# Projection sums of the state-space stage copied out of three PSUM banks by ScalarE

## The chip, the cores and the metric

The kernel runs on 1 core of one Trainium2 chip. The metric is the device time of one execution in microseconds; of several runs the median counts. Engines are named TensorE (PE in the profile, PEld for its weight loads), VectorE (DVE), ScalarE (ACT), GpSimd (POOL) and SyncE (SP, which issues DMAs).

## The reference

One layer of a hybrid decoder: an S5 state-space branch and a dilated-window attention branch work side by side on the same normalised input, for a prompt of 1024 rows and for 8 x 4 decode rows with a cache of 1024 keys.

```python
def _layer(h, h0_re, h0_im, attend, norm_in_g, w_in, ...):
    proj = _rmsnorm(h, norm_in_g) @ w_in            # (rows, 1024) @ (1024, 3072)
    x_s, z_s = proj[..., :o1], proj[..., o1:o2]     # 512 columns each, as the four below
    q, k, v, z_a = proj[..., o2:o3], proj[..., o3:o4], proj[..., o4:o5], proj[..., o5:]
    y_s, st_re, st_im = _s5_scan(x_s, h0_re, h0_im, A_re, A_im, log_dt, B_re, B_im, C_re, C_im, D)
    gl = gelu(y_s) @ w_glu + b_glu
    y_s = gl[..., :D_SSM] * sigmoid(gl[..., D_SSM:])
    y_s = _rmsnorm(y_s * silu(z_s), norm_ssm_g)
    y_a = _rmsnorm(attend(qh, kh, vh) * silu(z_a), norm_attn_g)
    return h + concatenate([y_s, y_a], axis=-1) @ w_out, kh, vh, st_re, st_im
```

The prompt's keys and values, the decode rows' keys and values, and the final states are outputs too (`k_prompt` is one of them).

## The kernel before

The first stage, from 0 to about 318 us, loads x, projects it with most of `w_in` and runs the state-space scan. Its instructions are ordered by a scheduler that simulates the engines and emits, engine by engine, one queue; what stands in the program text in another order may be interleaved. The later stages (rest of the projections, decode attention, prompt attention, output projection) are ordered by hand.

**PSUM.** In the first stage the eight banks are divided by use (L113): two for projection sums ("mm"), two for transposes ("tp"), two for the sums of the scan ("ss") and two for its outputs ("so"). A tile of a use takes the bank that was used longest ago, and its first matmul waits for the last reader of what lay there.

**Exact products by splitting.** The helper `split` makes of a value a rounded high part (ScalarE, L139 or L142) and the remainder (VectorE, L140 or L143). A product of two values is three matmuls: high x high, high x low, low x high.

**x load.** Eight chunks of 128 rows of the prompt, then 32 decode rows (`xd`), are normalised (ScalarE's square sum, VectorE's short root, GpSimd's scaling) and turned: four transposes by TensorE into a "tp" bank (L274; L281 for the decode rows), the high part by ScalarE, the remainder by VectorE, both from the bank into `xT`. Between the turns TensorE runs L294, the first weight block, whose matmuls use each chunk as it comes. Over the same stretch VectorE and ScalarE work out the constants of the scan (L429 to L555: powers, sines, the matrices bb and bbw).

**Projection.** Blocks of 256 columns of `w_in` are loaded, scaled and split into eight tiles `win`, in a pool of twelve buffers (L142 on ScalarE, L143 on VectorE). A block of state-space inputs, gates, queries or keys is two half blocks of 128 columns by three column ranges of 352: six sums of 24 matmuls each (L314), each 128 x 352 in one "mm" bank. Of a gate sum ScalarE takes a tanh (L341) and VectorE multiplies (L342; L344 for the decode columns of the first range), both reading the bank. Of a query or key sum ScalarE takes the high part (L378), VectorE the remainder (L379), a third copy goes to `k_prompt` for keys (L384), and all read the bank. The decode columns are copied to `pdT` (L363) and later turned into a "tp" bank (L405). The blocks in the order of the scan's steps are `((0, 1), (1, None), (2, 5), (3, 2), (4, 3), (5, 7), (6, 4), (7, 9))`, the pair being a step and the block that goes with it: 0 and 1 are state-space inputs, 2 and 3 gates, 4 and 5 queries, 7 keys, 8 and 9 values.

**Scan.** Eight steps run between the sums. A step's matrix `wa` is made by GpSimd and VectorE (L598), turned ("tp", L602) and split (`wl`); products with `uhl` fill "ss" banks; VectorE and GpSimd rotate and scan them (L644 to L677: `rc`, `rs`, `zz`, `zs`, `xx`); the splits `xhl`, `fhl`, `thl` feed the output sums L688 ("so").

Of the kernel before, what the change touches and what calls it, by code (L numbers as in the profile page):

```python
# [10 lines left out]
F32 = mybir.dt.float32  # L11
F32R = mybir.dt.float32r
I32 = mybir.dt.int32
AF = mybir.ActivationFunctionType
# [7 lines left out]
DB, DS = 8, 4  # L22
# [81 lines left out]
def hymba_kernel(ctx: ExitStack, tc: tile.TileContext, I, O):  # L104
    nc = tc.nc
    V, S, GP, T, SY = nc.vector, nc.scalar, nc.gpsimd, nc.tensor, nc.sync
# [3 lines left out]
    st = ctx.enter_context(tc.tile_pool(reuse_waits="tile", name="st", bufs=2))  # L110
    pst = ExitStack()
    ps = [pst.enter_context(tc.tile_pool(reuse_waits="tile", name="ps", bufs=1, space=PSUM))]
    banks = {"mm": 2, "tp": 2, "ss": 2, "so": 2}  # L113
    dr = ctx.enter_context(tc.tile_pool(reuse_waits="tile", name="dr", bufs=1, space=DRAM))

    def ps_tile(shape, tag, dt=F32):
# [2 lines left out]
    def mm_ps(shape):  # L119
        return ps_tile(shape, "mm")  # L120

    def tp_ps(shape):
        return ps_tile(shape, "tp")
# [10 lines left out]
    def f(t):  # L134
        return t.bitcast(F32)
# [74 lines left out]
    sp = pa.enter_context(tc.tile_pool(reuse_waits="tile", name="sp", bufs=1))  # L210
# [23 lines left out]
    with tc.tile_pool(reuse_waits="tile", name="xin", bufs=6) as xp:  # L234
# [15 lines left out]
        p = mm_ps([128, 512])  # L250
# [6 lines left out]
        pw = p  # L257
        for i in range(8):
# [11 lines left out]
            for h in range(2):  # L270
                p = tp_ps([128, 4, 128])
# [7 lines left out]
        p = tp_ps([128, 8, 32])  # L279
# [30 lines left out]
    def proj_t(p, w, c, x):  # L310
        n = 0
        for kt in range(8):
            for a, b in PASSES:
                T.matmul(p, w(b, kt)[:, c * 128:c * 128 + 128], x(a, kt), start=(n == 0), stop=(n == 23))  # L314
                n += 1

    def in_proj_s(reg, half, w):

        for c in range(2):
            ct = 2 * half + c  # L320

            t = sp.tile([128, 8, W + DB], F32, tag="stp", name="stp", bufs=2)
            if reg == 0:
                GP.memset(t[:, DS:, NC:W], 0.0)
                GP.memset(t[:, :DS, W:], 0.0)
            for k in range(3):
                p = mm_ps([128, 512])[:, :352]
                proj_t(p, w, c, lambda a, kt: xT[a][:, kt, 352 * k:352 * k + 352])
                d = 0 if k else NT
                c0 = (352 * k + d - NT) // 8  # L330
                n = (352 - d) // 8
                x = p[:, d:].rearrange("p (k s) -> p s k", s=8)
                rows = p[:, :d].rearrange("p (j b) -> p j b", b=DB)
                if reg == 0:
                    S.activation(t[:, :, c0:c0 + n], x, AF.Copy)
                    if d:
                        S.activation(t[:, :DS, NC:W], rows, AF.Copy)
                        V.tensor_copy(t[:, DS:, W:], rows)
                    continue
                e = st.tile([128, 512], F32, tag="ev", name="ev", bufs=3)[:, :352]  # L340
                S.activation(e, p, AF.Tanh, scale=0.5)  # L341
                V.scalar_tensor_tensor(t[:, :, c0:c0 + n], e[:, d:].rearrange("p (k s) -> p s k", s=8), 1.0, x, op0=OP.add, op1=OP.mult)  # L342
                if d:
                    V.scalar_tensor_tensor(t[:, :DS, NC:W], e[:, :d].rearrange("p (j b) -> p j b", b=DB), 1.0, rows, op0=OP.add, op1=OP.mult)  # L344
            if reg == 0:
                SY.dma_start(d_u[ct], t)
            else:
                SY.dma_start(d_gs[ct, :, :DS], t[:, :DS, :W])
                SY.dma_start(d_gs[ct, :, DS:, :NC], t[:, DS:, :NC])

    def in_proj_t(reg, half, w):

        pdT = wp.tile([128, 2, NT], F32, tag="pdT", name="pdT", bufs=2)
        for c in range(2):
            ct = 2 * half + c
            for k in range(3):
                pw = mm_ps([128, 512])[:, :352]
                proj_t(pw, w, c, lambda a, kt: xT[a][:, kt, 352 * k:352 * k + 352])
                d = 0 if k else NT
                p, n = pw[:, d:], 352 - d  # L360
                ts = slice(352 * k + d - NT, 352 * k + 352 - NT)
                if k == 0:
                    S.activation(pdT[:, c], pw[:, :NT], AF.Copy)  # L363
                    if reg == 2:
                        SY.dma_start(d_qT[ct], pdT[:, c])
                if reg == 5:
                    if half:
                        e = f(wp.tile([128, 2, 256], F32R, tag="w", name="ge", bufs=12)).rearrange("p a b -> p (a b)")
                    else:
                        e = st.tile([128, 512], F32, tag="ev", name="ev", bufs=3)  # L370
                    e = e[:, :n]
                    S.activation(e, p, AF.Tanh, scale=0.5)
                    V.scalar_tensor_tensor(e, e, 1.0, p, op0=OP.add, op1=OP.mult)
                    SY.dma_start(d_ga[ct, :, ts], e)
                    continue
                d_t = (d_q, d_k)[reg - 2]
                hi, lo = (st.tile([128, 512], F32R, tag="ev", name="eq", bufs=3)[:, :n] for _ in range(2))
                S.activation(hi, p, AF.Copy)  # L378
                V.tensor_tensor(out=lo, in0=p, in1=f(hi), op=OP.subtract)  # L379
                SY.dma_start(d_t[0, ct, :, ts], f(hi))  # L380
                SY.dma_start(d_t[1, ct, :, ts], f(lo))
                if reg == 3:
                    e = st.tile([128, 512], F32, tag="ev", name="ek", bufs=3)[:, :n]
                    S.activation(e, p, AF.Copy)  # L384
                    SY.dma_start(O["k_prompt"][ct, :, ts], e)
        return pdT

    def in_proj(blk, w=None):
# [323 lines left out]
    banks = {}  # L712
# [563 lines left out]
    def own_ops(o, t0):  # L1276

        shn = [64, 2, DS, E]

        def own(u):  # L1280
            def fn():
                if u == 0:
                    o.on = gk([128, 512], "vh", bufs=VH)[:64, :256].rearrange("p (j e) -> p j e", e=E)
                r = slice(2 * u, 2 * u + 2)
                m = row(64).rearrange("p (j k e) -> p j k e", j=2, k=DS)
                V.tensor_tensor(out=m, in0=sc[:, r, 288:292].unsqueeze(3).to_broadcast(shn), in1=o.v.unsqueeze(1).to_broadcast(shn), op=OP.mult)
                V.tensor_reduce(out=o.on[:, r], in_=m.rearrange("p j k e -> p j e k"), op=OP.add, axis=AX.X)
            return fn

        a = op(VE, 1.2, own(0), t0, [], take=["vh", "dm"], give=["dm"])  # L1290
        a = op(VE, 1.2, own(1), t0, [a], take=["dm"], give=["dm"])
        closed = op("", 0.0, lambda: d3.close(), t0, [a])

        def out():
            for j in range(DS):
                SY.dma_start(d_on[j].rearrange("b (h e) -> (b h) e", e=E), o.on[:, j])
        a = op(DM, 1.9, out, t0, [a], give=["vh"])
        return closed, op(DM, 0.5, lambda: SY.dma_start(yad, d_on.rearrange("j b c -> (j b) c")), t0, [a])
# [394 lines left out]
    closed, b = own_ops(soft, 8)  # L1693
# [67 lines left out]
    for s in range(8):  # L1761
# [3 lines left out]
        for hf in range(2):  # L1765
            p = (tp_ps if s % 2 else ss_ps)([128, 512])
# [112 lines left out]
```

## Time and profile before

| what | value |
|---|---|
| runs | 730.73, 731.66, 736.60 us; median 731.66 us |
| profiled execution | 736.03 us, its span 734.2 us |
| TensorE busy | 683.1 us, 93% of the span; mean granted clock 0.954 of full speed |
| VectorE busy | 540.3 us, 74% |
| ScalarE busy | 358.7 us, 49% |
| GpSimd busy | 329.2 us, 45% |
| moved by DMA | 116.29 MB |

The span runs from the first to the last instruction; the execution's time is 1.8 us longer. The profiled execution is 4.4 us above the median of the runs. A busy share is a mean over stages: the wait that ends last in a stage tells what bounds it. A row of a timeline has the start in us, the busy time in us, the engine, the line and the operation, tile written <- tiles read, and in brackets the idle time ahead of it with what ended that.

### The profile page before, as it was taken

How to read it: one execution, taken by the hardware profiler on the slowest of the kernel's cores; microseconds unless marked ns; L12 is line 12 of the kernel's file. 1: busy time of each engine (PE TensorE's matmuls, PEld its weight loads, DVE VectorE, ACT ScalarE, POOL GpSimd, SP SyncE). 2: the span in 40 equal slices, each digit the busy share in tenths (PEclk: the TensorE clock that was granted, in tenths of full speed). 3: DMA queues.
4: the chain of work that ended last, by engine and by line, in shares of the span. 5: the costliest groups of instructions: out<-in, count | busy, mean ns of one | idle time of the engine just before them, and what ended most of it. 6: DMA issues, size and time to landing. Idle time of an engine off the chain costs nothing.

```text
span 734.2 us, 12740 instructions
## 1 busy us (share of the span) xinstructions
PE 683.1 (93%) x4286; PEld 624.6 (85%) x4286; DVE 540.3 (74%) x1225; ACT 358.7 (49%) x802; POOL 329.2 (45%) x307
## 2 busy tenths in 40 slices
PE   7999999969799899998989898989999999899995
PEld 5999979969689899998989897868787778787995
DVE  5997859777698586334596678769899999884385
ACT  6663242414134334244252343268788987662263
POOL 2426456445473652201557571045666776330032
PEclk9999978989899999999999999999999999999998
DMA  8622432222324453168876764398978585126123
GB/s 273 214 61 80 147 100 88 80 79 69 96 61 121 155 164 126 52 219 261 242 237 197 236 211 166 109 259 245 289 250 251 166 262 148 37 71 223 57 93 144
DMA packets 79058, 116.29 MB, mean 158 GB/s; under 512 B 15728, under 2 KB 45424, under 8 KB 78992
## 3 DMA queue, kind: packets, MB, share of 16 engines
q1 hardware_dynamic: 78992, 115.47, 50.4%
q8 instruction: 34, 0.56, 0.3%
q14 instruction: 32, 0.26, 0.1%
HBM read 83.63 MB, written 30.62 MB: 156 GB/s over the span
## 4 chain that ended last, share of the span: by engine, by line
PE 53%; DVE 17%; DMA 11%; POOL 6%; issue 6%; SPq 3%; ACT 2%; DVEq 0%; POOLq 0%; ACTq 0%
PE mm L314 14%; PE mm L294 6%; PE fo L1665 4%; PE ops L1570 4%; POOL dm L981 4%; PE ss L294 3%; PE tp L294 3%; DMA ct<-in_cache_k_dram 3%; PE tp L1555 3%; PE so L688 3%; PE ss L1513 2%; PE fo L1376 2%; DMA dq<-d_pd 2%; DVE pm L1516 2%; DVE win L143 2%
## 5 line engine op out<-in xcount | busy, mean ns | idle before, releaser
L314 PE MATMUL mm<-xT,win 128*128 128x352 f32 x1008 | 179.8, 335 | 12.6 <-DVE eq L379 5.8
L314 PEld LDWEIGHTS mm<-xT,win 128*128 128x128 f32 x1008 | 168.1, 196 | 14.8 <-DVE eq L379 6.1
L1026 PE MATMUL mm<-xT,win 128*128 128x352 f32 x432 | 79.1, 339 | 3.2 <-DVE win L1008 3.2
L1026 PEld LDWEIGHTS mm<-xT,win 128*128 128x128 f32 x432 | 72.9, 198 | 4.1 <-DVE win L1008 3.9
L981 POOL TENSOR_TENSOR dm<-ct,dq 128x512 f32<-128x512 f32 x40 | 51.9, 1323 | 49.5 <-DMA ct<-in_cache_k_dram 31.8
L1536 POOL TENSOR_SCALAR pm<-pm,rd 128x128 f32<-128x128 f32 (+3 forms) x64 | 49.6, 777 | 49.8 <-DVE rd L1532 45.3
L1528 ACT ACTIVATE pm<-pm,mn 128x128 f32<-128x128 f32 (+3 forms) x64 | 49.4, 772 | 11.3 <-DVE mn L1516 10.4
L1562 DVE TENSOR_TENSOR pl<-tp,ph 128x512 fp32r<-128x512 f32 (+1 forms) x80 | 49.8, 628 | 6.5 <-ACT ph L1559 6.3
L1665 PE MATMUL fo<-wo,gh 128*128 128x512 f32 x192 | 53.0, 419 | 0.0
L294 PE MATMUL mm<-win,xT 128*128 128x256 f32 x384 | 50.9, 287 | 0.0
L813 PE MATMUL gl<-yh,wg 128*128 128x272 f32 (+1 forms) x256 | 50.0, 294 | 0.0
L1559 ACT ACTIVATE ph<-tp 128x512 fp32r<-128x512 f32 (+1 forms) x80 | 43.3, 546 | 11.5 <-PE tp L1555 6.4
L294 PEld LDWEIGHTS mm<-win,xT 128*128 128x128 f32 x384 | 47.2, 190 | 0.4 <-ACT xT L139 0.3
L1555 PE MATMUL tp<-ident,pm 128*128 128x128 f32 x288 | 45.5, 276 | 0.4 <-DVE yp L1592 0.3
L143 DVE SCALAR_TENSOR_TENSOR win<-wst,gin,win 128x256 fp32r<-128x256 f32 x72 | 43.6, 648 | 2.6 <-ACT win L142 2.4
L1665 PEld LDWEIGHTS fo<-wo,gh 128*128 128x128 f32 x192 | 36.1, 198 | 6.9
L813 PEld LDWEIGHTS gl<-yh,wg 128*128 128x128 f32 x256 | 41.6, 196 | 0.0
L1555 PEld LDWEIGHTS tp<-ident,pm 128*128 128x128 f32 x288 | 34.3, 141 | 6.4 <-PE ops L1570 0.8
L1516 DVE CUSTOM_DVE_ANT_0 pm<-ss,maskp 128x512 f32<-128x512 f32 (+2 forms) x64 | 36.5, 578 | 4.2 <-PE ss L1513 4.1
L984 DVE TENSOR_REDUCE scd<-dm 128x8 f32<-128x512 f32 x40 | 27.1, 681 | 16.4 <-POOL dm L981 16.2
L1513 PE MATMUL ss<-ka,qt 128*128 128x512 f32 (+2 forms) x96 | 35.8, 374 | 2.8 <-DMA ka<-d_k 1.9
L813 PE MATMUL gl<-yl,wg 128*128 128x272 f32 (+1 forms) x128 | 37.3, 291 | 0.0
(412 smaller groups left out, 1607.1 us busy)
## 6 DMA issues: line engine op xcount, KB each, us to landing
wst<-in_w_in_dram SPq DMA_DIRECT2D x24, 512.0 KB
ct<-in_cache_k_dram SPq DMA_DIRECT2D x48, 256.0 KB
ct<-in_cache_v_dram SPq DMA_DIRECT2D x48, 256.0 KB
xt<-in_x_prompt_dram SPq DMA_DIRECT2D x8, 512.0 KB
wst<-in_w_out_dram SPq DMA_DIRECT2D x8, 512.0 KB
xres<-in_x_prompt_dram SPq DMA_DIRECT2D x8, 512.0 KB
qt<-d_q SPq DMA_DIRECT2D x32, 128.0 KB
qw<-d_q SPq DMA_DIRECT2D x32, 128.0 KB
```

Source lines behind the costliest of these rows:

```text
L143: V.scalar_tensor_tensor(lo, src, scale, f(hi), op0=OP.mult, op1=OP.subtract)
L294: T.matmul(out, lhs(a, kt), w(b, kt)[:, c0:c0 + cn], start=(n == 0), stop=(n == 3 * ktn - 1))
L314: T.matmul(p, w(b, kt)[:, c * 128:c * 128 + 128], x(a, kt), start=(n == 0), stop=(n == 23))
L813: T.matmul(p, wg[:, b, kt, c:c + 128], o.y[a][:, kt, :, :o.w], start=(n == 0), stop=(n == 11))
L981: GP.tensor_tensor(out=y.m, in0=y.c, in1=x.q, op=OP.mult)
L1026: T.matmul(x.p, o.w[kt][:, b, c * 128:c * 128 + 128], xT[a][:, kt, 352 * k:352 * k + 352], start=(kt == 0 and j == 0), stop=(kt == 7 and j ...
L1513: T.matmul(x.p[c][:, :w], q[:, i % 4 * 128:i % 4 * 128 + 128], o.ka[:, 512 * c:512 * c + w], start=(m == 0), stop=(m == 1))
L1516: V.tensor_tensor_reduce(out=x.pm[:, 512 * c:512 * c + w], in0=x.p[c][:, :w], in1=maskp[:, (7 - i) * 128 + 512 * c:(7 - i) * 128 + 512 * c ...
L1536: a = op(PO, 0.02 + n * 0.0012, lambda: GP.tensor_scalar(x.pm[:, :n], x.pm[:, :n], x.rd, 1.0, op0=OP.mult, op1=OP.mult), pr, [a], give=["rd"])
L1555: T.transpose(x.p[:, n * 128:n * 128 + 128], o.rows[2 * m + u].pm[:, j * 128:j * 128 + 128], ident)
L1562: V.tensor_tensor(out=x.l[:, :w], in0=x.p[:, :w], in1=f(x.h[:, :w]), op=OP.subtract)
L1665: T.matmul(o.f[hf], o.g[u][:, i, k], wo[0][:, j, 2 * u + k, hf * 512:hf * 512 + 512], start=(u + k + n == 0), stop=(u + k + n == 4))
```

## The change

The banks for projection sums go from two to three, those for transposes from two to one. A new helper `raw` copies a sum of 128 x 352 from its bank into one of four SBUF buffers with ScalarE. Gates, queries and keys of the first stage are worked out from that copy, and the keys' copy is itself what is stored to `k_prompt`. State-space inputs (blocks 0 and 1) are read from the bank as before. In the changed kernel the lines behind L314 have other numbers: L341 is L349, L342 L350, L344 L352, L378 L388, L379 L389; lines of the scan are 8 higher.

```diff
-    banks = {"mm": 2, "tp": 2, "ss": 2, "so": 2}
+    banks = {"mm": 3, "tp": 1, "ss": 2, "so": 2}
...
+    def raw(p):
+
+        r = sp.tile([128, 352], F32, tag="raw", name="raw", bufs=4)
+        S.activation(r, p, AF.Copy)
+        return r
+
     def in_proj_s(reg, half, w):
...
-                e = st.tile([128, 512], F32, tag="ev", name="ev", bufs=3)[:, :352]
-                S.activation(e, p, AF.Tanh, scale=0.5)
+                r, e = raw(p), st.tile([128, 512], F32, tag="ev", name="ev", bufs=3)[:, :352]
+                x = r[:, d:].rearrange("p (k s) -> p s k", s=8)
+                rows = r[:, :d].rearrange("p (j b) -> p j b", b=DB)
+                S.activation(e, r, AF.Tanh, scale=0.5)
                 V.scalar_tensor_tensor(t[:, :, c0:c0 + n], e[:, d:].rearrange("p (k s) -> p s k", s=8), 1.0, x, op0=OP.add, op1=OP.mult)
...
                 proj_t(pw, w, c, lambda a, kt: xT[a][:, kt, 352 * k:352 * k + 352])
                 d = 0 if k else NT
+                if reg != 5:
+                    pw = raw(pw)
                 p, n = pw[:, d:], 352 - d
...
                 if reg == 3:
-                    e = st.tile([128, 512], F32, tag="ev", name="ek", bufs=3)[:, :n]
-                    S.activation(e, p, AF.Copy)
-                    SY.dma_start(O["k_prompt"][ct, :, ts], e)
+                    SY.dma_start(O["k_prompt"][ct, :, ts], p)
```

The scheduler puts some instructions elsewhere. VectorE's queue at the end of the x load, in the kernel before: `xT` are remainders of x (the one of 128x8x32 is that of the decode rows, the last), `tp`, `tn`, `tq`, `ex_q`, `cosk` are arithmetic for the scan's constants.

```order
L140 TENSOR_TENSOR xT_98<-tp,xT_97 128x4x128
L493 TENSOR_TENSOR tp<-tp,tq 128x544
L438 TENSOR_SCALAR ex_q<-ex_q 128x64
L140 TENSOR_TENSOR xT_98<-tp,xT_97 128x8x32
L494 TENSOR_SCALAR tp<-tp 128x544
L437 TENSOR_TENSOR ex_q<-ex_q,ex_r 128x64
L283 CAST xT_97<-xT_98 128x8x32
```

The same place in the changed kernel; `bb` and `bbw` are the scan's input matrices, the last of its constants, and `win` is a weight remainder.

```order
L534 TENSOR_TENSOR fi<-t_1007,den 128x32
L544 TENSOR_SCALAR t_1007<-fi,sg 128x32
L545 TENSOR_SCALAR t_1008<-fi,sgn 128x32
L548 TENSOR_TENSOR tm<-bsw,t_1007 128x512
L549 TENSOR_TENSOR bb<-bb,tm 128x512
L140 TENSOR_TENSOR xT_98<-tp,xT_97 128x4x128
L548 TENSOR_TENSOR tm<-bst,t_1008 128x512
L549 TENSOR_TENSOR bbw<-bbw,tm 128x512
L140 TENSOR_TENSOR xT_98<-tp,xT_97 128x8x32
L283 CAST xT_97<-xT_98 128x8x32
L143 SCALAR_TENSOR_TENSOR win<-wst,gin,win 128x256 x7
```

In the kernel before, the constants go on behind the last remainder of x, up to the second `bbw` (there L541); in the changed one all of them stand ahead of it.

The second place is the start of a sum on TensorE, the fifth of the first block of queries, in the kernel before (a semaphore in brackets is what an instruction waits for; `mm_1819` and `mm_1850` are successive sums):

```order
L314 MATMUL mm_1819<-xT0_97,win_1687 128x352 x2
L314 MATMUL mm_1819<-xT1_98,win_1687 128x352
L314 MATMUL mm_1850<-xT0_97,win_1666 128x352 [waits DVE_49]
L314 MATMUL mm_1850<-xT0_97,win_1666 128x352
L314 MATMUL mm_1850<-xT1_98,win_1666 128x352
```

And the same sums in the changed kernel, `mm_1827` and `mm_1860`:

```order
L314 MATMUL mm_1827<-xT0_97,win_1687 128x352 x2
L314 MATMUL mm_1827<-xT1_98,win_1687 128x352
L314 MATMUL mm_1860<-xT0_97,win_1666 128x352
L696 MATMUL so_1505<-xhl_1476,fhl_1408 128x136 [waits Activation_49]
L696 MATMUL so_1505<-xhl_1476,fhl_1408 128x136 x2
```

Before, the sum's first matmul waits for VectorE; now it carries no wait, and the output sums of a scan step (`so`) stand behind it.

The third place is VectorE's queue at the end of the same block, in the kernel before:

```order
L140 TENSOR_TENSOR thl<-tpl,thl 128x4x128
L143 SCALAR_TENSOR_TENSOR win<-wst,gin,win 128x256 x2
L379 TENSOR_TENSOR eq<-mm,eq 128x352
L143 SCALAR_TENSOR_TENSOR win<-wst,gin,win 128x256
L598 TENSOR_TENSOR wa<-wa,wb 128x512
L140 TENSOR_TENSOR uhl<-u,uhl 128x4x144
L342 SCALAR_TENSOR_TENSOR stp<-ev,mm 128x8x40
```

And in the changed kernel:

```order
L140 TENSOR_TENSOR fhl<-f_1542,fhl 128x4x128
L606 TENSOR_TENSOR wa<-wa,wb 128x512
L140 TENSOR_TENSOR thl<-tpl,thl 128x4x128
L143 SCALAR_TENSOR_TENSOR win<-wst,gin,win 128x256
L140 TENSOR_TENSOR uhl<-u,uhl 128x4x144
L143 SCALAR_TENSOR_TENSOR win<-wst,gin,win 128x256 x5
L685 SCALAR_TENSOR_TENSOR xx<-zz,sg,xx 128x4x128
L143 SCALAR_TENSOR_TENSOR win<-wst,gin,win 128x256 x2
L389 TENSOR_TENSOR eq<-raw,eq 128x352
```

Before, the difference that frees a bank (`eq`) stands among the last of the weight remainders, five of which stand ahead of this piece; now it reads `raw`, and the block's eight remainders stand together with more of the scan's operations ahead of them.

## Rows read from the trace of the kernel before

**Rows 1.** Costliest groups: line, engine, operation, tiles, shape, count | busy us, mean ns | idle before

```profile
L314 PE MATMUL mm<-xT,win 128*128 128x352 f32 x1008 | 179.8, 335 | 12.6 <-DVE eq L379 5.8
```

**Rows 2.** TensorE's waits, 0 to 320 us: us in total, times, longest us

```profile
PE mm L314 <- DVE eq L379: 5.8, 1, 5.8
PE mm L314 <- DVE stp L342: 5.4, 2, 4.8
PE so L688 <- ACT xhl L139: 2.4, 2, 1.8
```

**Rows 3.** Windows: stretch, us, busy per engine (instructions), TensorE's clock, DMA share, GB/s

```profile
17.00:46.40 29.40, 28.23 (x242) 27.71 (x241) 28.45 (x111) 18.92 (x41) 12.57 (x14) 1.00 0.46 150
46.40:312.00 265.60, 249.10 (x1626) 235.04 (x1624) 192.29 (x325) 96.11 (x229) 130.09 (x109) 0.94 0.33 101
...
150.00:155.00 5.00, 1.85 (x6) 1.85 (x7) 5.00 (x7) 0.00 (x0) 3.14 (x3) 0.66 0.24 70
155.00:160.00 5.00, 5.00 (x24) 4.98 (x24) 1.40 (x3) 0.62 (x3) 2.67 (x2) 0.65 0.25 90
...
190.00:195.00 5.00, 3.32 (x12) 3.32 (x13) 4.67 (x9) 1.45 (x4) 0.00 (x0) 0.50 0.49 131
```

The engines in a row stand in the order PE, PEld, DVE, ACT, POOL.

**Rows 4.** The chain that ended last, end of the first stage: start us, us, what

```profile
313.13 4.71 PE mm L294 x39
...
320.18 7.05 DMA wst<-in_w_glu_dram
```

**Rows 5.** Timeline, 148 to 153.5 us

```profile
148.02 1.75 DVE L140 TENSOR_TENSOR thl<-tpl,thl 128x512 fp32r<-128x512 f32 x1
149.27 1.61 POOL L676 TENSOR_TENSOR zz<-zs,rs 64x512 f32<-64x512 f32 x1
149.69 2.98 DVE L143 SCALAR_TENSOR_TENSOR win<-wst,gin,win 128x256 fp32r<-128x256 f32 x2
...
152.59 0.51 DVE L379 TENSOR_TENSOR eq<-mm,eq 128x352 fp32r<-128x352 f32 x1
...
153.15 0.66 PE L314 MATMUL mm<-xT,win 128*128 128x352 f32 x1 [5.83 <-DVE eq L379]
```

**Rows 6.** Timeline of VectorE and TensorE, 180 to 192 us

```profile
180.91 7.85 DVE L143 SCALAR_TENSOR_TENSOR win<-wst,gin,win 128x256 fp32r<-128x256 f32 x6
188.69 1.85 DVE L677 SCALAR_TENSOR_TENSOR xx<-zz,sg,xx 128x512 f32<-128x512 f32 x1
...
191.68 1.25 PE L314 MATMUL mm<-xT,win 128*128 128x352 f32 x3 [4.80 <-DVE stp L342]
```

**Rows 7.** Timeline of VectorE, then TensorE, 44 to 62 us

```profile
44.30 0.42 DVE L140 TENSOR_TENSOR xT<-tp,xT 128x256 fp32r<-128x256 f32 x1
44.64 0.43 DVE L494 TENSOR_SCALAR tp<-tp 128x544 f32<-128x544 f32 x1
...
49.93 0.49 DVE L143 SCALAR_TENSOR_TENSOR win<-wst,gin,win 128x256 fp32r<-128x256 f32 x1
50.33 0.22 DVE L440 TENSOR_TENSOR mags<-ex_q,ex_i 128x64 f32<-128x64 f32 x1
...
61.06 0.69 DVE L541 TENSOR_TENSOR bbw<-bbw,tm 128x512 f32<-128x512 f32 x1
...
46.48 0.80 PE L314 MATMUL mm<-xT,win 128*128 128x352 f32 x4
```

**Rows 8.** Instructions of 46.4 to 312 us: duration ns min/median/max, or busy us, mean ns

```profile
L379 DVE TENSOR_TENSOR eq<-mm,eq x18: 465/514/526, 118.3 to 289.8; 128x352 fp32r<-128x352 f32 x12, 128x320 fp32r<-128x320 f32 x6
L598 DVE TENSOR_TENSOR wa<-wa,wb x8: 675/1318/1785, 74.3 to 272.0; 128x512 f32<-128x512 f32 x8
...
L143 DVE SCALAR_TENSOR_TENSOR win<-wst,gin,win 128x256 fp32r<-128x256 f32 x60 | 37.2, 661 | 1.9 <-ACT win L142 1.6
L378 ACT ACTIVATE eq<-mm 128x352 fp32r<-128x352 f32 x12 | 5.5, 460 | 10.7 <-PE mm L314 9.6 <-ACT yo L689 0.6 <-DMA d_k<-eq 0.5
L384 ACT ACTIVATE ek<-mm 128x352 f32<-128x352 f32 x4 | 1.8, 454 | 2.6 <-DVE eq L379 2.6
```

## Prediction

> **What bounds the kernel now.** I read the costliest groups first, then TensorE's waits, then its windows, then the timelines around its longest waits. The 1008 matmuls of L314, the transposed projections, are the largest group: 179.8 us busy, 12.6 us of idle ahead of them, put down to VectorE [rows 1]. The waits of the first 320 us say where: one of 5.8 us for a difference at L379 and two, 5.4 us together, for a gate product at L342 [rows 2]. Both instructions read a PSUM sum and so free its bank. The windows give the clock: from 46.4 to 312 us TensorE is busy 249.10 of 265.60 us at a granted 0.94, while VectorE is busy 192.29 us and ScalarE only 96.11 [rows 3]. So the stage is bound by TensorE, with some 16.5 us of holes and a clock that is not full. The end of the stage carries over: its last sums lead straight into the load of w_glu in the chain that ended last [rows 4], so I carry a gain or loss of this stage 1:1 to the end.
>
> **Part 1: copies out of three banks (the gain).** 147 to 153 us: VectorE runs a split of 1.75 us, then two weight remainders in 2.98 us, and only then, at 152.59, the 0.51 us difference that frees the bank; the next matmul starts at 153.15 after 5.83 us of waiting [rows 5]. 181 to 191 us: six weight remainders of 7.85 us and a product of 1.85 us stand ahead of the L342 product, and the matmul waits 4.80 us [rows 6]. After the change a sum's bank is freed by a copy on ScalarE, and a third bank lies between, so neither wait can happen in this form: 5.83 + 4.80 = 10.6 us. Behind each hole the granted clock is low: 0.65 with TensorE busy 5.00 us, 0.66 with 1.85 us, 0.50 with 3.32 us [rows 3]. The work lost against full clock is 5.00 x 0.35 + 1.85 x 0.34 + 3.32 x 0.50 = 4.0 us; it goes if the holes go. Gain: 14.6 us, bounds 0 (see part 3) and 19 (with the 0.6 and 1.4 us of small bank waits that remain of the 12.6, and with the 2.4 us that matmuls wait for xhl [rows 2]).
>
> **Part 2: one bank for transposes (the loss).** The queue of VectorE decides this, and it is plain in the order. Before, the remainders of x (xT, L140) stand close together, the last one with setup arithmetic of the state-space stage (L494 to L541) still behind it; after, the transposes of one chunk need the remainder of the chunk just before, the scheduler fills the time with that arithmetic, and the last remainder stands behind all of it. An engine works its queue in order. In the trace of before the last remainder runs at 44.30, the arithmetic from 44.64 to 61.06 + 0.69 = 61.75: 17.1 us [rows 7]. Not all of it moves ahead: eight weight remainders (0.40 us each from start to start, the pace of 49.93 to 50.33), which stay behind, are 3.2 us; the conversion L283, the sum L413, the copy L338 and one idle piece of 0.50 us are, from starts in the same timeline, about 0.2 + 0.35 + 0.1 + 0.5 = 1.15 us. So 17.1 - 3.2 - 1.15 = 12.8 us more work stands ahead of the last remainder, and VectorE has no slack for it: between 17 and 46.4 us it was busy 28.45 of 29.40 us [rows 3]. The first matmul of L314, at 46.48 in the trace of before [rows 7], then starts near 59.3. TensorE had no idle time to give in 17 to 46.4 (28.23 us busy, [rows 3]) and its work does not shrink, so the delay counts in full. I add 0.2 us for four ScalarE instructions of that arithmetic that now stand between two copies of x; the bounds are +11 (VectorE a little faster where GpSimd is quieter) and +15 (the four instructions, 2.6 us, fully in the way). I take +13.
>
> **Part 3: what is late next.** The weights' remainders (L143) and the operands of the state-space sums are made on the same VectorE queue, which is as full as before. In the order at the first of the two places, one fhl, wa, thl and uhl, six remainders, a product xx and two remainders stand one behind the other, where a sum of 24 matmuls takes 24 x 0.335 = 8.0 us. With the mean of 0.661 us eight remainders are 5.3 us [rows 8], and the chain's operations among them (wa 1.32 by its median [rows 8], thl 1.75 by the row at 148.02 [rows 5], xx 1.85 by the row at 188.69 [rows 6], the other two counted like thl at most) up to 8 us: 13 us in all. The tiles of the next block become free over the last sum of the old one (8.0 us) and the pool has four tiles ahead, which last four eighths of a sum (4.0 us). So 12 us are there for 13, and a wait of 1 to 3 us is left at such a place. I take 2 us at each of two places: +4, bounds 0 and +14.6 (the hole moves as a whole from the bank to the weights).
>
> **Part 4: the engines' own work.** ScalarE gets 30 copies (12 gate sums, 18 of queries and keys) at the 0.460 us of L378, and loses 6 copies for k_prompt of 0.454 us [rows 8]: 13.8 - 2.7 = 11.1 us on an engine that is idle two thirds of the stretch [rows 3]. It hides; if ScalarE were late, a bank would be held some 0.46 us longer, with a spare bank to cover that. VectorE: 18 differences and 12 gate products now read two SBUF operands. With a PSUM operand the difference took 465 to 526 ns in all 18 cases, whatever GpSimd did; wa, with two SBUF operands, took from 675 to 1785 ns [rows 8]. So a new price exists that the trace of before shows only on its neighbours: below, 0 (or a tenth of a microsecond less for each of the 30, were PSUM the slower operand: -3 on VectorE); above, the median excess of wa, 1.318 - 0.675 = 0.64 us each, 30 x 0.64 = 19 us on VectorE. As GpSimd is busy for 130.09 of 265.60 us [rows 3], I take half, 9 us. They lie beside TensorE's work, except where TensorE waits for that queue (part 3); on the path I count 0, bounds -1 and +5.
>
> The Trainium skill speaks against this part ("SBUF — State Buffer", section "SBUF: two separate sides"): VectorE and GpSimd share a port pair as an exclusive lock, held for a whole instruction, and the loser blocks. The spread of wa beside the flat difference [rows 8] agrees; by that rule a blocked difference waits up to a whole GpSimd instruction, 1.61 us in a row of that stretch [rows 5], and that is the rival "slower" below.
>
> **Sum.** -14.6 + 13 + 4 + 0 = +2.4 us on the profiled execution's 736.0 us. That execution stands 4.4 us above the median of 731.66, and carries the same terms, so the median would come to 734.1; I say 734. This is a change that moves two large terms of opposite sign, and 1% (7.3 us) is about what a measurement tells from no change.
>
> **Rivals.**
> *Faster (0.27).* The bank was the only tie between the two engines that mattered. Then nearly all holes after the x load go, not only two: 16.5 us, and the clock gap of 249.10 x 0.06 = 15 us closes by half to all; against the delay of 13 us this is -11 to -18, say 721. For it: sums in the new order start on a ScalarE signal or on none. Against it: 2.4 us of the holes are waits for xhl, whose chain the change doesn't shorten [rows 2], and some of the low clock follows those.
> The Trainium skill ("Perfetto Trace Analysis", section "Matmuls") has independent groups rotate through different banks, so that emptying one overlaps the next; it speaks for the sums and against the transposes, which lose just that.
> *Slower (0.30).* VectorE's queue is the bind and not the bank: the matmul that waited for a bank waits for a weight remainder or for xhl at nearly the same time, because the same six to eight remainders at 1.3 us each (7.85 us for six [rows 6]) stand ahead, now lengthened by two-operand work that GpSimd blocks. Of the 14.6 us some 3 are kept: 13 - 3 = +10, about 742. It decides where VectorE's work between two block starts exceeds the 12 us of part 3, which 9 us more over some eight blocks brings near. For it: VectorE was busy all of 150 to 155 us [rows 3]. Against it: the arithmetic of part 2 is gone from behind 46 us, which gives VectorE 12.8 us back early on.
> *The change doesn't do what it says (inside the two outer cases).* The x load keeps its pace, because VectorE gets through the arithmetic in gaps that the trace doesn't show: -14.6 + 4 = -10.6, about 721. Or ScalarE, which also splits weights, makes its copies late, and banks are held as before: +13, about 745.
>
> **How the numbers follow.** My forecast has 0.43 and lies with its own range, 727 to 739 (loss +11 to +15, holes +1 to +8, gain 12 to 17), inside the band of no measurable change. Faster has 0.27, slower 0.30. The range that leaves out no more than two in ten reaches from most of the faster case to the slower one: 720 to 746.
>
> **What would show it.** The first matmul of L314 (at its new line) at 58 to 61 us instead of 46.5, and VectorE's last xT remainder at about 57; TensorE about two thirds busy in 17 to 59 us; no wait of the sums for a difference or a gate product; waits for win or xhl of 1 to 3 us near block starts; a granted clock at or above 0.96 behind the x load; new copies of 0.46 us on ScalarE; differences at L389 with a spread up to a microsecond or more. I am wrong if L314 starts before 52 us (then it is faster), if the waits for weights and xhl sum to over 10 us (then it is slower), or if the end of the stage moves and the end of the kernel doesn't.

## The result, and the profile after

The changed kernel took 742.74 us (median of 4 runs, 739.86 to 747.09) beside 733.16 us of the kernel before: a ratio of 1.0134, 95% interval 1.0088 to 1.0180. Measured again with six runs of its own and 17 of before it was 1.0144 (1.0103 to 1.0185). So it is slower by about 1.4%, some 10 us. The forecast was 734 us with a range of 720 to 746: the range holds the time, the likeliest case (no measurable change) was not the one that came.

The costliest groups of the profile after (columns as in [rows 1]):

```profile
L314 PE MATMUL mm<-xT,win 128*128 128x352 f32 x1008 | 176.3, 330 | 2.2 <-DVE win L143 2.2
...
L294 PE MATMUL mm<-win,xT 128*128 128x256 f32 x384 | 53.8, 293 | 2.6 <-ACT xT L139 2.5
```

The idle time ahead of L314 has fallen from 12.6 us [rows 1] to 2.2, and none of it is due to a difference or a gate product any more. The waits of TensorE in the first 330 us show what came instead (us in total, times, longest):

```profile
PE so L696 <- DVE xhl L140: 5.2, 3, 2.3
PE ss L630 <- DVE f L618: 3.6, 1, 3.6
PE so L696 <- ACT xhl L139: 2.9, 4, 1.1
PE mm L294 <- ACT xT L139: 2.5, 2, 2.1
PE mm L314 <- DVE win L143: 2.2, 2, 2.0
...
PE ss L418 <- DVE xT L283: 1.6, 1, 1.6
```

The bank waits of [rows 2] are gone; the scan's operands xhl and f, made by VectorE (a part of xhl by ScalarE), are late instead. Part of the wait for xhl is old: before, there were the 2.4 us of [rows 2] and these:

```profile
PE so L688 <- DVE xhl L140: 1.4, 1, 1.4
```

The windows (columns as in [rows 3]) of the x load and of the stretch from the first sum of L314 to the last value sum:

```profile
17.00:60.30 43.30, 33.52 (x252) 30.38 (x252) 40.88 (x148) 22.24 (x44) 13.65 (x17) 0.97 0.32 102
60.30:324.30 264.00, 248.40 (x1673) 235.14 (x1672) 189.06 (x288) 104.80 (x251) 134.94 (x110) 0.97 0.34 103
```

The x load is 13.9 us longer than the 29.4 us of [rows 3], with 252 matmuls for 242: TensorE is busy 33.52 of 43.30 us, and VectorE has 12.4 us more to do (40.88 for 28.45). The same stretch of the kernel before, 46.5 to 317.8 us, reads

```profile
46.50:317.80 271.30, 254.80 (x1674) 240.75 (x1673) 192.19 (x325) 96.58 (x231) 130.85 (x112) 0.94 0.33 101
```

so behind the x load this execution is 7.3 us shorter, with nearly the same idle time (264.0 - 248.4 = 15.6 us, before 16.5) and a higher granted clock (0.97, before 0.94); the stage ends 6.5 us later. The execution profiled before (736.03 us) was among the slowest of its kernel's runs, the one after (740.28 us) among the fastest. Their granted clocks over the whole span, 0.954 and 0.973, are not typical either: the median is 0.964 over 17 further runs of before and 0.963 over six of the change. So the higher clock belongs to these two executions and is not shown for the change. In another profiled execution of the changed kernel, of 744.80 us, the same stretch reads

```profile
59.70:326.10 266.40, 251.44 (x1673) 237.51 (x1672) 189.46 (x288) 104.83 (x251) 136.06 (x110) 0.96 0.33 102
```

that is 4.9 us shorter than before, and the stage ends 8.3 us later.

The end of the x load in the timeline after answers to [rows 7]:

```profile
58.94 0.69 DVE L549 TENSOR_TENSOR bbw<-bbw,tm 128x512 f32<-128x512 f32 x1
...
59.55 0.42 DVE L140 TENSOR_TENSOR xT<-tp,xT 128x256 fp32r<-128x256 f32 x1
59.74 1.40 POOL L650 TENSOR_TENSOR rc<-cosk 128x512 f32<-128x512 f32 x1
60.00 5.35 DVE L283 CAST xT<-xT 128x256 fp32r<-128x256 f32 x1
61.11 1.40 POOL L653 TENSOR_TENSOR rs<-cosk,sink 128x512 f32<-128x512 f32 x1
62.48 1.40 POOL L650 TENSOR_TENSOR rc<-cosk 128x512 f32<-128x512 f32 x1
63.84 1.35 POOL L653 TENSOR_TENSOR rs<-cosk,sink 128x512 f32<-128x512 f32 x1
...
60.28 0.97 PE L314 MATMUL mm<-xT,win 128*128 128x352 f32 x5
```

The last remainder of x stands behind bbw, the last of the constants, and L314 starts at 60.28 instead of 46.48. And the differences and gate products, now with two SBUF operands (ns, min/median/max):

```profile
L389 DVE TENSOR_TENSOR eq<-raw,eq x18: 479/526/1619, 129.0 to 296.5; 128x352 fp32r<-128x352 f32 x12, 128x320 fp32r<-128x320 f32 x6
...
L350 DVE SCALAR_TENSOR_TENSOR stp<-ev,raw x12: 730/842/2101, 168.7 to 235.4; 128x352 f32<-128x352 f32 x8, 128x320 f32<-128x320 f32 x4
```

The same product in the kernel before:

```profile
L342 DVE SCALAR_TENSOR_TENSOR stp<-ev,mm x12: 714/791/857, 154.7 to 224.8; 128x352 f32<-128x352 f32 x8, 128x320 f32<-128x320 f32 x4
```

The medians have hardly moved. The longest have: 1619 ns for a difference that never took more than 526 [rows 8], and 2101 ns for a product that never took more than 857.

### The profile page after: what moved, and what is told of

It reads as the page before. It is cut to its first block, busy times and chain, and to the rows that moved or that the text cites. A ratio compares the mean times of both kernels' runs of the same rounds, so it can differ in the third digit from the quotient of the medians.

```text
span 738.5 us, 12739 instructions
## 1 busy us (share of the span) xinstructions
PE 677.6 (92%) x4286; PEld 617.8 (84%) x4286; DVE 549.0 (74%) x1225; ACT 369.9 (50%) x826; POOL 334.1 (45%) x307
## 5 line engine op out<-in xcount | busy, mean ns | idle before, releaser
L314 PE MATMUL mm<-xT,win 128*128 128x352 f32 x1008 | 176.3, 330 | 2.2 <-DVE win L143 2.2
L314 PEld LDWEIGHTS mm<-xT,win 128*128 128x128 f32 x1008 | 165.1, 192 | 3.0 <-DVE win L143 2.8
L1034 PE MATMUL mm<-xT,win 128*128 128x352 f32 x432 | 77.7, 334 | 4.4 <-DVE win L1016 3.1
L1034 PEld LDWEIGHTS mm<-xT,win 128*128 128x128 f32 x432 | 71.5, 195 | 5.6 <-DVE win L1016 3.9
L294 PE MATMUL mm<-win,xT 128*128 128x256 f32 x384 | 53.8, 293 | 2.6 <-ACT xT L139 2.5
L294 PEld LDWEIGHTS mm<-win,xT 128*128 128x128 f32 x384 | 48.8, 194 | 3.7 <-ACT xT L139 3.6
L143 DVE SCALAR_TENSOR_TENSOR win<-wst,gin,win 128x256 fp32r<-128x256 f32 x72 | 38.3, 577 | 6.2 <-ACT win L142 6.1
```

The lines of the kernel that those rows point to most:

```text
L294: T.matmul(out, lhs(a, kt), w(b, kt)[:, c0:c0 + cn], start=(n == 0), stop=(n == 3 * ktn - 1))
L1034: T.matmul(x.p, o.w[kt][:, b, c * 128:c * 128 + 128], xT[a][:, kt, 352 * k:352 * k + 352], start=(kt == 0 and j == 0), stop=(kt == 7 and j ...
```

## The experiments

Two theories stood at the start. A: the change is two terms, one transpose bank that costs the x load its whole delay, and copies that gain. B: the x load's delay is largely made up behind it, and the loss is VectorE's work with two SBUF operands. The ratios are to the kernel before, with 95% intervals, each against 17 to 29 runs of it. Where two ratios are subtracted below, both intervals enter; joined (the root of the sum of squares, an estimate), they leave about half a per cent, 3 to 4 us, on either side of the difference.

**Three banks for sums, one for transposes, no copies.**

```diff
 (kernel before)
-    banks = {"mm": 2, "tp": 2, "ss": 2, "so": 2}
+    banks = {"mm": 3, "tp": 1, "ss": 2, "so": 2}
```

> The kernel before with three banks for sums and one for transposes, no copies. Theory A (one transpose bank costs the x load some 13 us, whatever else is done): L314 starts near 60 us instead of 46.5, the time is 738 to 746 us. Theory B (the x load's delay is made up later, since the arithmetic is out of the way; the loss is VectorE's two-operand work beside GpSimd): 731 to 736 us, as there are no copies here.

Measured: 737.12 us, ratio 1.0074 (1.0044 to 1.0105); L314 starts at 60.64 us. The time lies between the two forecasts. Its waits behind the x load:

```profile
PE mm L314 <- DVE win L143: 4.3, 3, 2.0
PE so L688 <- DVE xhl L140: 3.7, 2, 2.4
```

No wait of the sums for a bank is left, though VectorE still reads the bank: the third bank does by itself what the copies were there for.

**Copies alone, banks two and two.**

```diff
 (changed kernel)
-    banks = {"mm": 3, "tp": 1, "ss": 2, "so": 2}
+    banks = {"mm": 2, "tp": 2, "ss": 2, "so": 2}
```

> The changed kernel with two banks for sums and two for transposes again, copies kept. Theory A: L314 starts at 46 to 48 us, bank waits are gone or under 3 us, some 6 to 8 us faster than before: 725 to 728 us. Theory B: VectorE's differences and products are as long as in the changed kernel (mean about 0.9 and 1.1 us) and the time is 735 to 742 us.

Measured: 735.47 us, ratio 1.0025 (0.9995 to 1.0055), L314 from 47.22 us. Bank waits are gone (0.4 us for a copy), and waits for f (5.3 us) and win (4.7 us) stand in their place. Theory A's 725 to 728 is out.

**The change with a fast x load.** The scan's output banks lie idle during the x load.

```diff
 (changed kernel)
-                p = tp_ps([128, 4, 128])
+                p = (so_ps if h else tp_ps)([128, 4, 128])
```

> The changed kernel, but every second turn of the x load goes into a bank of the scan's outputs, which lie idle then; banks three and one as in the change. Theory A: L314 starts at 46 to 48 us, the rest as in the changed kernel, 725 to 729 us. Theory B: the arithmetic stands behind the x load again, waits for f and xhl grow, 736 to 742 us.

Measured: 738.49 us, ratio 1.0068 (1.0036 to 1.0101). L314 starts at 46.24 us, so the x load's loss is undone, but only some 0.8% of the change's 1.4% comes back. Theory A in its simple form falls.

**The change again.**

> The changed kernel once more, unaltered, beside the others on one chip. Both theories: the time of the first measurement, 738 to 745 us; its distance to the run with three banks and no copies (737.1 us) is the price of the copies: 3 to 7 us by theory B (VectorE's two-operand work), 0 to 2 us by theory A.

Measured: 745.50 us, ratio 1.0144 (1.0103 to 1.0185). Against three banks without copies (1.0074) the copies cost 0.70% (0.2 to 1.2%), about 5 us.

**Remainders on GpSimd.**

```diff
 (changed kernel)
-                V.tensor_tensor(out=lo, in0=p, in1=f(hi), op=OP.subtract)
+                (V if reg == 5 else GP).tensor_tensor(out=lo, in0=p, in1=f(hi), op=OP.subtract)
```

> The changed kernel with the 18 remainders of queries and keys on GpSimd instead of VectorE (they read only SBUF now). Theory B: VectorE loses 16.0 us of busy time and the waits for xhl, f and win shrink; 3 to 8 us faster than the changed kernel, 734 to 739 us. Theory A: VectorE's queue isn't the matter, the time is within 2 us of the changed kernel's, or worse as GpSimd's products come later.

Measured: 751.48 us, ratio 1.0242 (1.0209 to 1.0276). Theory B's 734 to 739 is missed; theory A had left room for a worse time, without a number. The windows from the first sum of L314 on:

```profile
59.30:330.70 271.40, 255.84 (x1673) 241.82 (x1672) 185.31 (x270) 104.41 (x251) 149.41 (x128) 0.94 0.33 100
```

VectorE's busy time falls by 3.8 us only (from 189.06): the 18 remainders took 16.0 us of it, and the other 270 instructions now take 12.2 us more. GpSimd's rises by 14.5. One gate product took 3158 ns. Relieving VectorE by loading the engine that blocks it does not tell the theories apart, and is no cure.

**Third bank, fast x load, no copies.** The edits of the first and the third run, on the kernel before.

> No copies, three banks for sums, one for transposes, every second turn of the x load in an idle bank of the scan's outputs. Theory B: bank waits gone as with three banks alone, L314 starts at 46 to 48 us, but the scan's constants come late and holes before the scan's sums take part of it: 727 to 733 us. Theory A (the x load's 14 us come back whole on top of three banks alone): 722 to 725 us.

Measured: 730.96 us, ratio 0.9950 (0.9923 to 0.9976), L314 from 46.59 us: faster than before. Against the first run the x load's price is 1.0074 - 0.9950 = 1.24%, 9 us; against the third, the copies' is 1.0068 - 0.9950 = 1.18%.

**VectorE reads the bank, ScalarE the copy.** This splits "the copies" into ScalarE's instructions and VectorE's operands.

```diff
 (third run's kernel)
-                x = r[:, d:].rearrange("p (k s) -> p s k", s=8)
-                rows = r[:, :d].rearrange("p (j b) -> p j b", b=DB)
...
+                bank = pw
                 if reg != 5:
                     pw = raw(pw)
...
-                V.tensor_tensor(out=lo, in0=p, in1=f(hi), op=OP.subtract)
+                V.tensor_tensor(out=lo, in0=bank[:, d:], in1=f(hi), op=OP.subtract)
```

> The third run's kernel (copies, turns of the x load in two kinds of bank) with ScalarE still working from the copies, but VectorE's 18 differences and 16 gate products reading the PSUM bank as before; a bank is then held until VectorE has read it. If the copies cost time because VectorE's two SBUF operands are blocked by GpSimd, the differences come back to 465 to 526 ns, the products to 714 to 870, and the time to 729 to 734 us. If the cost lies in ScalarE's 30 further instructions and the half microsecond that each product or difference starts later, it stays at 736 to 740 us.

Measured: 725.65 us, ratio 0.9892 (0.9857 to 0.9928): 1.76% below the third run. All five engines' queues hold the same instructions in the same order in these two kernels; 34 operands differ, and with them the moment at which a bank is free, which now waits for VectorE again. Against the sixth run, which has no copies, this one is 0.58% lower (0.1 to 1.0%): ScalarE's copies by themselves cost nothing here. The difference and the product here:

```profile
L388 DVE TENSOR_TENSOR eq<-mm,eq x18: 475/511/525, 120.4 to 281.6; 128x352 fp32r<-128x352 f32 x12, 128x320 fp32r<-128x320 f32 x6
...
L348 DVE SCALAR_TENSOR_TENSOR stp<-ev,mm x12: 771/800/858, 155.4 to 220.5; 128x352 f32<-128x352 f32 x8, 128x320 f32<-128x320 f32 x4
```

The windows of the same stretch, first of the third run's kernel, then of this one:

```profile
46.20:321.30 275.10, 262.35 (x1673) 246.70 (x1672) 196.13 (x325) 106.28 (x255) 134.01 (x112) 0.92 0.32 99
```

```profile
46.90:310.00 263.10, 253.99 (x1674) 239.38 (x1673) 192.64 (x325) 106.37 (x255) 130.07 (x112) 0.95 0.34 104
```

12.0 us shorter: 8.4 us of that is TensorE's busy time, at a granted clock of 0.95 instead of 0.92, and 3.6 us is idle time (12.75 to 9.11). So two thirds of the price of the SBUF operands is paid through the clock, in these two executions. One hole of the third run's kernel shows the way there:

```profile
150.08 4.53 POOL L682 TENSOR_TENSOR xx<-zs,rc 128x512 f32<-128x512 f32 x1 [3.49 <-DVE zs L676]
...
157.37 1.96 DVE L685 SCALAR_TENSOR_TENSOR xx<-zz,sg,xx 128x512 f32<-128x512 f32 x1 [3.91 <-POOL zz L684]
...
160.98 0.44 PE L696 MATMUL so<-xhl,fhl 128*128 128x136 f32 x2 [3.05 <-ACT xhl L139]
```

Here it is GpSimd that is late: its scan product takes 4.53 us, VectorE then waits 3.91 us for GpSimd, and TensorE 3.05 us for the operand made from it. The windows from there on (TensorE's clock is the third number from the end):

```profile
155.00:160.00 5.00, 2.92 (x19) 2.63 (x17) 2.63 (x2) 0.64 (x3) 4.86 (x4) 1.00 0.00 0
160.00:165.00 5.00, 3.08 (x15) 1.81 (x15) 4.30 (x5) 1.68 (x5) 2.35 (x2) 0.67 0.02 3
165.00:170.00 5.00, 5.00 (x26) 3.94 (x26) 0.03 (x1) 1.16 (x3) 1.70 (x3) 0.50 0.48 136
170.00:175.00 5.00, 5.00 (x24) 5.00 (x22) 4.33 (x5) 1.20 (x3) 2.42 (x2) 0.50 0.12 31
175.00:180.00 5.00, 5.00 (x22) 5.00 (x22) 4.42 (x11) 0.96 (x2) 2.08 (x3) 0.63 0.29 74
```

In the seventh run this product takes at most 1.72 us (in the kernel before one of eight took 3.04), and the clock is 1.00 from 115 to 185 us.

**One output bank instead of one transpose bank.**

```diff
 (kernel before)
-    banks = {"mm": 2, "tp": 2, "ss": 2, "so": 2}
+    banks = {"mm": 3, "tp": 2, "ss": 2, "so": 1}
```

> The kernel before with three banks for sums, two for transposes, and one instead of two for the scan's outputs, no copies. If the third bank alone is what helps, and one output bank costs the scan little, 728 to 733 us with L314 from 46 to 48 us; if the scan's outputs wait for their bank (yo), waits of TensorE for yo of several us and 734 us or more.

Measured: 735.91 us, ratio 1.0054 (1.0021 to 1.0086). In the profiled execution, of 731.88 us (the shortest of its twelve), there is no wait for yo; waits for xhl are 8.3 us and for wa 3.8. The time says that the third bank isn't free here, but not by the mechanism expected; what makes xhl later was not followed up.

**The change with VectorE reading the bank.** The edit of the seventh run on the changed kernel; again every queue has the change's own order.

> The changed kernel with all its copies and its banks three and one, but VectorE's 18 differences and 16 gate products read the PSUM bank; every engine's queue has the same instructions in the same order as in the changed kernel. If the operand's place is a price of its own, as between the third and the seventh run (1.8%), this is 1 to 2% faster than the changed kernel, 728 to 736 us, with L314 still starting at 59 to 61 us; what is left to the seventh run (725.7 us) is then the x load's price, 4 to 10 us. If the seventh run's gain came from the fast x load together with the copies, it stays at 738 to 745 us.

Measured: 737.89 us, ratio 1.0058 (1.0026 to 1.0090), 0.86% (0.3 to 1.4%) below the change measured again; L314 starts at 59.04 us. The gain is a little short of the 1 to 2% expected, the rest, 1.0058 - 0.9892 = 1.66%, is the x load's price, with whatever the other order of the queues behind it adds or gives back: 12.2 us, a little above the 4 to 10 expected. Its waits:

```profile
PE so L695 <- DVE xhl L140: 6.0, 2, 3.7
PE mm L294 <- ACT xT L139: 2.1, 1, 2.1
PE mm L314 <- DVE win L143: 2.0, 1, 2.0
```

Of the wait of 3.6 us for f 0.7 us is left.

**What the runs add up to.** With 1% as 7.33 us: a third bank with copies for ScalarE alone, -1.08% or -7.9 us (the seventh run); one transpose bank in the x load, +1.66% or +12.2 us (ninth against seventh); VectorE's operands in SBUF, +0.86% or +6.3 us (the change again against the ninth). The sum, +10.6 us, is by construction the change's 1.44%; that the terms interact is seen in the operands' price with the fast x load, 12.9 us instead of 6.3 (the gap of 0.90% is just clear of noise: 0.2 to 1.6%). Why it is twice as large there is open: the constants' arithmetic then stands behind the x load on the same queue, but no run took that apart.

## Why the prediction was right or wrong

**The copies and the third bank (part 1): right.** Both bank waits went. With the new waits that I set against them (part 3) I had -14.6 + 4 = -10.6 us, and the seventh run, which has these edits without the two losses, measured -7.9. By the first run the third bank alone is enough for the bank waits. The 4.0 us of clock in my 14.6 came from an execution whose clock, 0.954, lay below its kernel's median of 0.964.

**The x load (part 2): right, in place and size.** +13 us was forecast from VectorE's queue, L314 near 59.3; it started at 60.28 (13.8 later), and 12.2 us is what the x load costs in time between the ninth and the seventh run. The step rested on an order and one row: a queue busy 28.45 of 29.40 us has no room for 12.8 us of arithmetic moved ahead of the last remainder, and its busy time there grew by 12.4 us. That it is not made up later, as theory B had it, is shown by that pair; the pair of the first and sixth runs gives 9 us and the pair of the change and the third run 5.6, where VectorE's operands blur it.

**What is late next (part 3): the right queue, the wrong waiter and size.** I expected weights at block starts, 4 us. The weights cost 2.2 us; xhl and f cost 5.2 + 2.9 + 3.6 = 11.7 us, of which 2.4 + 1.4 = 3.8 us of waits for xhl had been there before: 7.9 us are new. Idle time as a whole stayed where it was (15.6 for 16.5 us), so most of the first 10.6 us of the gain came back as other holes. My sign for "slower", waits for weights and xhl of over 10 us together, came: 2.2 + 5.2 + 2.9 = 10.3.

**VectorE's operands (part 4): the step that failed.** I put VectorE's extra time at 9 us. From the means of one execution it is 12 x (975 - 519) + 6 x (724 - 480) + 8 x (1146 - 814) + 4 x (810 - 740) ns = 5.5 + 1.5 + 2.7 + 0.3, or 9.9 us unrounded, the means being those of the two shapes of each operation after and before. That was right. What failed is the sentence that they "lie beside TensorE's work" and count 0 on the path with +5 at most: the price is 6.3 us in the change and 12.9 us with the fast x load. VectorE's queue is the one that TensorE waits for after the banks are freed, so what is added there can be on the path. I had also looked only at what VectorE loses. GpSimd loses too: in the third run's stretch it is busy 134.01 us, in the seventh's 130.07, and GpSimd's products stand in the chain that makes xhl. With this term at 6.3 my sum would have been +8.7; with 7.9 for the 10.6 us that my gain and new waits leave, and 12.2 for 13 us of x load, it comes to the +10.6 of the runs.

The timeline after shows the blocking itself, VectorE and GpSimd from 134 to 138 us:

```profile
134.19 1.71 POOL L682 TENSOR_TENSOR xx<-zs,rc 128x512 f32<-128x512 f32 x1 [1.87 <-DVE zs L676]
...
134.68 1.60 DVE L389 TENSOR_TENSOR eq<-raw,eq 128x352 fp32r<-128x352 f32 x1
...
135.98 1.43 POOL L683 TENSOR_TENSOR zz<-zs,rs 64x512 f32<-64x512 f32 x1
...
136.20 0.68 DVE L140 TENSOR_TENSOR wl<-tp,wh 128x512 fp32r<-128x512 f32 x1
...
136.80 0.99 DVE L389 TENSOR_TENSOR eq<-raw,eq 128x352 fp32r<-128x352 f32 x1
```

The first difference starts within a GpSimd product and ends 0.38 us after it (134.68 + 1.60 = 136.28, the product at 134.19 + 1.71 = 135.90); the second ends 0.38 us after the next product (137.79 and 137.41). Between them a remainder with a PSUM operand takes its usual 0.68 us in the middle of a GpSimd instruction. The Trainium skill ("SBUF — State Buffer", section "SBUF: two separate sides") says that of a GpSimd instruction and a VectorE instruction with two SBUF inputs whichever starts first has the shared port pair for its whole length, and that the other blocks. These rows agree with it, and that a PSUM operand goes free is what the same rows show.

The other direction, from the same execution:

```profile
184.13 0.89 DVE L350 SCALAR_TENSOR_TENSOR stp<-ev,raw 128x352 f32<-128x352 f32 x1
184.28 4.60 POOL L682 TENSOR_TENSOR xx<-zs,rc 128x512 f32<-128x512 f32 x1 [1.31 <-DVE zs L676]
184.91 0.71 DVE L140 TENSOR_TENSOR thl<-tpl,thl 128x512 fp32r<-128x512 f32 x1
...
187.49 0.23 DVE L352 SCALAR_TENSOR_TENSOR stp<-ev,raw 128x32 f32<-128x32 f32 x1
```

And the same instructions of the ninth run, where the gate product reads the bank:

```profile
181.27 0.83 DVE L348 SCALAR_TENSOR_TENSOR stp<-ev,mm 128x352 f32<-128x352 f32 x1
181.43 1.30 POOL L681 TENSOR_TENSOR xx<-zs,rc 128x512 f32<-128x512 f32 x1 [1.31 <-DVE zs L675]
182.01 1.26 DVE L140 TENSOR_TENSOR thl<-tpl,thl 128x512 fp32r<-128x512 f32 x1
```

With a gate product from SBUF just ahead of it, the GpSimd product ends 1.16 us after the last of a row of VectorE instructions that run from 184.13 to 187.72; with the gate product from PSUM it takes 1.30 us, and it is the next VectorE instruction that gets longer (1.26 for 0.71 us). That is how the operands reach the chain of the scan; how much of the price goes through GpSimd and how much through VectorE was not taken apart.

**The rivals.** "Slower" at +10 us, 742 us, hit the time, and its two causes both hold: the waits moved to xhl (and f, not to weights), lengthened by two-operand work. It let some 3 us of the 14.6 be kept; 7.9 - 6.3 = 1.6 us were. My chance of 0.30 for it was too low, because I gave the sum itself no share of a price that I had worked out; the stated range held the time only because this rival was in it. One sum of mine does not come out: loss +11 to +15, holes +1 to +8 and gain 12 to 17 reach from -5 to +11, so 727 to 743 and not 727 to 739. "The change doesn't do what it says" is out: the banks were freed, and the x load did not keep its pace.

The version that beats both kernels is the seventh run's: three banks, the x load's turns in two kinds of bank, ScalarE working from the copies and VectorE from PSUM, 725.65 us, 1.1% faster than before.

## What to carry to other kernels

A copy out of PSUM frees a bank, but an instruction of VectorE that then reads two SBUF operands can be blocked by what GpSimd is doing, and can block GpSimd in its turn: where GpSimd is busy half the time, leave VectorE's operand in PSUM and let only ScalarE work from the copy, or give the sums another bank. When a bank wait is removed, ask which queue the engine waits for next; work added to that queue is on the path, even where its engine is idle a quarter of the time. A bank taken from one use is paid where that use is dense: look there for what the scheduler puts into the gap, and use banks that lie idle in that phase.

## What was not expected of the hardware

In the change a conversion of 128 x 256 elements with one SBUF operand (L283) took 5.35 us, in the kernel before 0.28 us. Its row begins at 60.00, four GpSimd products run one behind the other from 59.74 to 65.19 us, and it ends at 65.35: by these rows it lost to four instructions in a row, though it stood ready behind the first. The GpSimd product of 4.60 us above is the same thing the other way round. The same 5.34 us came in the first and ninth runs (5339 and 5337 ns), and 0.295 us in the third and seventh, where the conversion ran at 44.5 and 45.2 us. TensorE waited 1.6 us for it.

The other is how far the price of 34 operands went: 3.5 us less of VectorE's busy time in the stretch (196.13 to 192.64) and 3.9 us less of GpSimd's went with a stretch that is 12.0 us shorter, in two kernels with the same instructions in the same order.
